# The last part of an output norm: engine order taken from tables, and its last tile accumulated onto the residual in PSUM

## Chip, cores and metric

The kernel runs on one core of one Trainium2 chip. The metric is the device time of one execution in microseconds, the median of several runs; smaller is better.

## What is computed

One layer of a streaming encoder: Mamba-2 heads beside latent attention heads, then a dense SwiGLU FFN, over 512 + 64 = 576 token columns of width 1024. Only its end matters here: the last down-projection of the FFN, the residual, and the final RMS norm.

```python
def rmsnorm(x, w):
    xf = x.astype(jnp.float32)
    y = xf * lax.rsqrt(jnp.mean(xf * xf, axis=-1, keepdims=True) + EPS)
    return (y * w.astype(jnp.float32)).astype(x.dtype)
...
# end of the layer:  y = rmsnorm(x + down(silu(gate) * up), final_gain)
```

The kernel holds activations transposed: 8 channel tiles t = 0..7 of 128 channels (partitions) by 576 tokens (columns). The mean over channels is therefore a sum over partitions and over the 8 tiles. Partitions are summed on TensorE (PE) with a matrix of ones.

## The kernel before

The FFN's 22 blocks of 128 hidden channels run through PE at nearly full occupancy. The last four blocks are projected down at the very end, and this end is cut in two parts of token columns: part 0 has columns 0 to 319 and part 1 columns 320 to 575 (`parts`). For each part and each tile t, `down_half` (L1101) issues 12 matmuls (4 blocks, each as three products of high and low halves of weight and activation) into one PSUM tile (`ps_l0_t` in part 0, `ps_l1_t` in part 1; the profile cuts both to `ps_l`). Then for each tile:

- VectorE (DVE) adds the PSUM tile to the residual in place, `add` (L1145): `x2[t] = ps + x2[t]`. In the rows x2 is `x`; `x2_0` holds the tiles 0 to 3, `x2_1` the tiles 4 to 7.
- ScalarE (ACT) squares it (L1184 in part 0, L1233 in part 1, result `sq`), and multiplies it in place by the norm's gain for that channel, `gain` (L1149). Tile 7 has no `gain`: its gain is multiplied in at the end.
- The squares are summed over tiles: in part 0 by GpSimd (POOL, L1189, tiles 0, 2, 4 into `ss`) and by DVE (L1194 into `sq_last`, joined to `ss` in two adds at L1192); in part 1 by POOL for the tiles 0 to 3 (L1238), while the tiles 4 to 7 are summed by PE itself, as `packed` (L1203) accumulates ones times `ss` and ones times each `sq` in PSUM.
- The norm's factor comes from `norm_steps` (L182 to L193): Ln, Exp and Square on ACT, three small operations on DVE. In part 0 the sum over partitions is the matmul at L1226; it stands behind tile 2 of part 1, and the factor is written back to PSUM (`ps_n`) and copied to SBUF (`R`, L1231). In part 1 the packed factor `Rp` is spread to all partitions by four matmuls (L1257, eight passes, result `ps_r`), with seven matmuls `ones` times `ones` (L1251, result unused) ahead of them, and one half is copied to SBUF (`R`, L1258).
- `outs` multiplies each tile by the factor: DVE (L1159; L1155 with the gain for tile 7), POOL for the tiles 0 and 1 of each part (L1157, factor from SBUF). The results are stored: part 0 from the SyncE (SP) queue in pairs, part 1 in single tiles by `SENDS`, four on SP and four on ACT's queue.

Two things set the order of work on an engine. Nearly all of the program is emitted in dependence order, and then tables of numbers (`ISSUE`, used in `issue_in_order`) give for PE, DVE, ACT, POOL and SP the order in which the emitted instructions are issued; tables called `PLACES` give the buffer that each tile takes. Part 1 stands in a block `tc.manual_schedule` (L1209) for PE, DVE, POOL and ACT: there these four engines issue in the order in which the code is written, and what the tables say of that stretch is just this order. Part 0 is under the tables.

Of the kernel before, what the change touches and what calls it, by code (L numbers as in the profile page):

```python
# [13 lines left out]
AF = mybir.ActivationFunctionType  # L14
ALU = mybir.AluOpType
# [4 lines left out]
P = 128  # L20
D = 1024
# [35 lines left out]
def hybrid_layer_kernel(ctx: ExitStack, tc: tile.TileContext, a, o):  # L57
# [54 lines left out]
    def col(c):  # L112
        return par[:, c : c + 1]
# [66 lines left out]
    def norm_steps(R, src, n, view=lambda z: z, eps=True):  # L180

        w = R.shape[1] if len(R.shape) == 2 else T  # L182
        y0, nv, u = (view(tmp(f"nr_{z}", w)) for z in "yvu")

        def first():
            act.activation(y0, src, AF.Ln, scale=1.0 / n, bias=epsb if eps else 0.0)
            dve.tensor_scalar(nv, src, -0.5 / n, -0.5 * EPS if eps else 0.0, ALU.mult, ALU.add)
            act.activation(y0, y0, AF.Exp, scale=-0.5)
            act.activation(u, y0, AF.Square)

        def second():
            dve.tensor_tensor(u, u, nv, ALU.mult)
            dve.scalar_tensor_tensor(R, u, 1.5, y0, ALU.add, ALU.mult)  # L193

        return first, second, nv
# [256 lines left out]
    def bank(tag, name):  # L452
        return placed(psq if tag == "sc" else psh, [P, 512], F32, tag, name)
# [646 lines left out]

    def down_half(ps, terms, cols, first=True, last=True):  # L1101
        for k, ((whi, wlo), (xhi, xlo)) in enumerate(terms):
            for i, (w, x) in enumerate(((whi, xhi), (whi, xlo), (wlo, xhi))):
                pe.matmul(  # L1104
                    ps, w, x[:, cols], start=first and k == 0 and i == 0, stop=last and k == len(terms) - 1 and i == 2,
                )
# [33 lines left out]
    def lbank(tag, name, i):  # L1140
        return bank(tag, name)[:, : parts[i].stop - parts[i].start]
# [9 lines left out]
    def outs(i, t, r, rp):  # L1151

        y = x2[t][:, parts[i]]
        if t == KT - 1:
            dve.scalar_tensor_tensor(y, y, col(C_NL + t), r, ALU.mult, ALU.mult)  # L1155
        elif t in POOLS[i]:
            pool.tensor_tensor(y, y, rp, ALU.mult)  # L1157
        else:
            dve.tensor_tensor(y, y, r, ALU.mult)  # L1159
# [35 lines left out]


    W1 = parts[1].stop - parts[1].start
    W2 = W1 // 2
# [9 lines left out]

    with tc.manual_schedule(engines={pe.engine, dve.engine, pool.engine, act.engine}):  # L1209
        pn0, pn1 = lbank("sc", "ps_n3_0", 0), bank("pp", "ps_n3_1")  # L1210
        first, second, _ = norm_steps(pn0, pn0, D, eps=False)
        q = []
        sent = [set(), set()]

        def out(i, k, r, rp):
            t = ORDERS[i][k]
            outs(i, t, r, rp)
            sent[i].add(t)
            if i == 0 and t ^ 1 in sent[i]:
                send(i, t & 6, 2, sp)  # L1220

        for t in range(KT):
            p = lbank(("hm", "sc", "pp")[t % 3], f"ps_l1_{t}", 1)
            down_half(p, last_terms(t), parts[1])
            if t == 2:
                pe.matmul(pn0, ones, ss3[:, parts[0]], start=True, stop=True)  # L1226
                first()
            add(t, 1, p)
            if t == 2:
                second()  # L1230
                act.copy(R3[:, parts[0]], pn0)  # L1231
            q.append(tmp("sq", W1))
            act.activation(q[t], x2[t][:, parts[1]], AF.Square)  # L1233
            if t < KT - 1:
                gain(t, 1)

            for k in {0: (), 1: (1, 0)}.get(t, (t,) if t < NP else ()):
                pool.tensor_tensor(ss3[:, parts[1]], ss3[:, parts[1]], q[k], ALU.add)  # L1238
            for k in OUTS.get(t, ()):
                out(0, k, pn0, R3[:, parts[0]])  # L1240
        packed(pn1, ss3[:, parts[1]], True, False)
        for t in range(NP, KT):
            packed(pn1, q[t], False, t == KT - 1)
        Rp = tmp("Rp", W2)
        first, second, _ = norm_steps(Rp, pn1[:, :W2], D, eps=False)
        first()
        second()

        warm = bank("hm", "ps_warm_last")
        for _ in range(7):  # L1250
            pe.matmul(warm[:, :P], ones, ones, start=True, stop=True)  # L1251

        pr1 = [lbank("sc", f"ps_r3_{z}", 1) for z in range(2)]
        for z in pr1:
            for hf in range(2):
                row = ident[:, 64 * hf : 64 * hf + 1].to_broadcast([P, P])
                pe.matmul(z[:, hf * W2 : (hf + 1) * W2], row, Rp, start=True, stop=True)  # L1257
        act.copy(R3[:, parts[1]], pr1[1])  # L1258
        for k in range(KT):
            out(1, k, pr1[0], R3[:, parts[1]])  # L1260
        for t, q in SENDS:
            send(1, t, 1, q)
    close(psH_)
# [10 lines left out]
def issue_in_order(tc, nc):  # L1274
# [26 lines left out]
    "sc": "".join("""  # L1301
021021202120120120120120120120120102102012102102102102121021021201201201201201210210210202102102021
""".split()),
    "pp": "".join("""
0210210212120102110201221002101210120121021012020120120120120120210210210210210210210210210210210210210210210210221012
0120210
""".split()),
# [130 lines left out]
4238 4170 4191 4198 4163 4192 4164 4193 4171-4172 4199 4165 4184 4200 4226 4173 4201 4174-4177 4239 4194 4227  # L1438
4207-4208 4228-4230 4240-4242 4202 4243 4231 4185 4209 4195 4262 4210 4186 4232 4211-4212 4263 4233 4213 4234 4214
4235 4244 4264 4203 4215 4223 4217 4204 4220 4245 4236 4218 4237 4216 4265-4266 4219 4224 4246 4267 4221 4225  # L1440
4250-4251 4268-4270 4247 4271 4252 4274 4253 4275 4254 4276-4277 4248 4255 4222 4278-4279 4272 4256 4249 4273
4257-4259 4280 4260-4261 4281-4391
""",
# [30 lines left out]
888 903 909 887 910 898-899 904 911 900 892 901 919 906 915 908 912 893 914 913 869 905 920-921 923 870 922 917 894  # L1474
918 924-925 916 895 928 902 927 937 926 929 896 938 932 931 939 930 933-934 940 935-936 941 946 942 944 943 945 947
951 949 948 954 950 952-953 955-979
""",
# [21 lines left out]
621 617-618 622 626 623 620 627-629 632 631 637 633-636 640 638-639 643 645 648 646 651 654 644 649 647 656 641 650  # L1499
657 655 659 658 663 660 642 661 664-665 652 666 662 674 667 669 653 675 670 668 677 676 671-672 686 673 684 680 678  # L1500
685 682 681 688-690 679 692 687 693-700 691 701-704 683 705-719
# [8 lines left out]
121 124-130 132 131 134 133 136 135 138 137 139-144 146 145 148 147 149-150 152 151 154 153 155-156 158 157 160 159  # L1510
161-169 171-172 170 175-176 174 177-181
""",
# [100 lines left out]
```

## Time and profile before

| quantity | value |
| --- | --- |
| median of 3 runs | 640.36 us (639.76 to 640.44) |
| the profiled execution's own time | 639.58 us |
| its span | 637.5 us |
| PE busy | 626.2 us (98% of the span) |
| DVE, ACT, POOL busy | 551.4, 390.4, 70.7 us |
| granted TensorE clock | 1.00 in the slices that hold part 0 and part 1 |

The span runs from the first to the last instruction of the execution; 639.58 - 637.5 = 2.08 us of the execution's own time lie around it. Times in a row of the timeline are counted from the start of the span: start, duration, engine, line, operation, result, sources, shapes, and in square brackets how long the engine had been idle before and what ended that. "x3" says that a row holds three instructions back to back. A duration contains the pipeline's fill, so the starts of rows lie closer together than their durations.

### The profile page before, as it was taken

Reading aid. Unit: us, or ns where it says so; the run is one execution under the profiler, and the core shown is the slowest. Engines: PE = TensorE matmul, PEld = TensorE weight load, DVE = VectorE, ACT = ScalarE, POOL = GpSimd, SP = SyncE. Lnnn points to the kernel's source line nnn. Section 1 sums busy time; section 2 is a strip of 40 time slices with the busy share of each in tenths; the row PEclk is TensorE's granted clock in tenths of the full one; section 3 lists DMA queues with packets and bytes.
Section 4 is the critical chain, followed back from the end, with each engine's and each line's share of the span. In section 5 each row is a group of like instructions: output and inputs, shape, how many; then the busy total and the mean of one; then the engine's idle time right before and its main releaser. Section 6 shows DMA issues by size and latency. Waiting matters only on the chain.

```text
span 637.5 us, 11950 instructions
## 1 busy us (share of the span) xinstructions
PE 626.2 (98%) x4639; PEld 598.0 (94%) x4639; DVE 551.4 (86%) x980; ACT 390.4 (61%) x751; POOL 70.7 (11%) x111
## 2 busy tenths in 40 slices
PE   9999999999999999999999999999999999999994
PEld 9899999985887899999999999999999999999994
DVE  6999996899867599999998997889888998998763
ACT  7655425789766479955656565655565656545463
POOL 1322122001010000000012002100211011100022
PEclk9999999999999999999999999999999999999999
DMA  9522185314131132231187427550765274723004
GB/s 310 207 51 78 35 209 151 114 30 147 72 111 34 62 131 73 93 108 67 36 202 158 128 91 163 141 136 40 189 159 133 67 182 111 181 74 133 1 1 149
DMA packets 31560, 72.66 MB, mean 114 GB/s; under 512 B 3706, under 2 KB 11400, under 8 KB 31248
## 3 DMA queue, kind: packets, MB, share of 16 engines
q1 hardware_dynamic: 25360, 60.77, 29.8%
q0 software_dynamic: 5424, 10.57, 9.3%
q8 instruction: 36, 0.59, 0.4%
q10 hardware_dynamic: 720, 0.57, 0.3%
q14 instruction: 20, 0.16, 0.1%
HBM read 58.03 MB, written 3.30 MB: 96 GB/s over the span
## 4 chain that ended last, share of the span: by engine, by line
PE 48%; issue 1%; DVE 1%; ACT 1%; POOL 1%; POOLq 0%; DVEq 0%
PE ps_x L894 17%; PE ps_dx L1034 9%; PE ps_z L894 9%; PE ps_dz L1034 5%; PE ps_y L894 4%; PE ps_dy L1034 2%; PE ps_l L1104 2%; POOL x L1157 0%; DVE x L1145 0%; DVE sq_last L1194 0%; DVE ss L1192 0%; POOL ss L1238 0%; POOLq L1600 0%; ACT sq L1233 0%; ACT x L1149 0%
## 5 line engine op out<-in xcount | busy, mean ns | idle before, releaser
L894 PE MATMUL ps_x<-xop,wh_gu_S 128*128 128x288 f32 x504 | 126.2, 295 | 0.0
L894 PEld LDWEIGHTS ps_x<-xop,wh_gu_S 128*128 128x128 f32 x504 | 88.2, 188 | 0.7 <-ACT u L963 0.2
L894 PE MATMUL ps_x<-xop,wl_gu_S 128*128 128x288 f32 x252 | 73.2, 295 | 0.0
L894 PE MATMUL ps_z<-xop,gu_a 128*128 128x288 f32 x252 | 61.7, 295 | 0.0
L127 ACT CAST wh_gu_S<-gu 128x1024 fp32r<-128x1024 f32 x44 | 46.2, 1053 | 14.8 <-PE ps_y L894 4.2
L128 DVE TENSOR_TENSOR wl_gu_S<-gu,wh_gu_S 128x1024 fp32r<-128x1024 f32 x44 | 52.8, 1217 | 0.8 <-ACT wh_gu_S L127 0.5
L894 PEld LDWEIGHTS ps_x<-xop,wl_gu_S 128*128 128x128 f32 x252 | 47.1, 188 | 0.0
L1047 POOL DMA_DIRECT2D x<-db x16 | 14.9, 930 | 277.9 <-ACT db L1040 247.8
L143 PE MATMUL ps_in<-xs,wh_in 128*128 128x288 f32 x256 | 45.5, 298 | 0.0
L894 PE MATMUL ps_y<-xop,wh_gu_A 128*128 128x288 f32 x168 | 44.9, 295 | 0.0
L894 PEld LDWEIGHTS ps_z<-xop,gu_a 128*128 128x128 f32 x252 | 43.5, 188 | 0.0
L894 PE MATMUL ps_z<-xop,wh_gu_S 128*128 128x288 f32 x168 | 43.4, 295 | 0.0
L894 PE MATMUL ps_x<-xop,wh_gu_A 128*128 128x288 f32 x168 | 42.7, 295 | 0.0
L143 PEld LDWEIGHTS ps_in<-xs,wh_in 128*128 128x128 f32 x256 | 37.8, 189 | 0.2
L127 ACT CAST wh_gu_A<-gu 128x1024 fp32r<-128x1024 f32 x22 | 23.1, 1051 | 23.0 <-PE ps_x L894 16.1
L894 PEld LDWEIGHTS ps_y<-xop,wh_gu_A 128*128 128x128 f32 x168 | 30.1, 188 | 0.1
L894 PEld LDWEIGHTS ps_z<-xop,wh_gu_S 128*128 128x128 f32 x168 | 29.7, 188 | 0.0
L128 DVE TENSOR_TENSOR wl_gu_A<-gu,wh_gu_A 128x1024 fp32r<-128x1024 f32 x22 | 26.8, 1217 | 3.3 <-ACT wh_gu_A L127 1.8
L894 PEld LDWEIGHTS ps_x<-xop,wh_gu_A 128*128 128x128 f32 x168 | 29.5, 188 | 0.0
L465 PE MATMUL ps_o<-cat_y,wh_out 128*128 128x288 f32 x128 | 29.0, 312 | 0.0
L143 PE MATMUL ps_in<-xs,wl_in 128*128 128x288 f32 x128 | 27.5, 296 | 0.0
L465 PE MATMUL ps_o<-cat_o,wh_out 128*128 128x288 f32 x128 | 27.3, 297 | 0.0
(594 smaller groups left out, 2002.8 us busy)
## 6 DMA issues: line engine op xcount, KB each, us to landing
gu<-in_w_gu SPq DMA_DIRECT2D x44, 512.0 KB, 4.8
db<-in_w_down SPq DMA_DIRECT2D x16, 512.0 KB, 4.5
x<-db POOLq DMA_DIRECT2D x16, 288.0 KB, 6.5
x<-dc POOLq DMA_DIRECT2D x16, 288.0 KB, 4.1
wr_in<-in_w_in SPq DMA_DIRECT2D x8, 512.0 KB, 6.2
wr_out<-in_w_out SPq DMA_DIRECT2D x8, 512.0 KB, 3.3
cumb<-cumD SPq DMA_DIRECT2D x5, 512.0 KB, 5.0
x<-in_xT SPq DMA_DIRECT2D x2, 1152.0 KB, 6.6
```

What stands on the lines that cost most here:

```text
L127: act.copy(hi, raw)
L128: dve.tensor_tensor(lo, raw, hi.bitcast(F32), ALU.subtract)
L143: pe.matmul(ps[:m, hf, :n], w, x[:, hf * n : (hf + 1) * n], start=start and k == 0 and i == 0, stop=stop and k == last and i == 2,)
L465: pe.matmul(ps[:, :n], w, x[:, cols], start=not onto and k == 0 and i == 0, stop=onto or (k == len(terms) - 1 and i == 2), skip_group_chec ...
L894: pe.matmul(ps, p, q, start=not onto and first and kp == kps[0] and j == 0, stop=onto or (last and kp == kps[-1] and j == 2), skip_group_c ...
L1034: pe.matmul(ps, l, r, start=not onto and k == 0 and j == 0, stop=onto or (k == n - 1 and j == 2), skip_group_check=onto,)
L1047: pool.dma_start(x2[t], v, accum_op=ALU.add)
L1104: pe.matmul(ps, w, x[:, cols], start=first and k == 0 and i == 0, stop=last and k == len(terms) - 1 and i == 2,)
```

## The change

Four edits, all in the last part of the program.

1. The `manual_schedule` block is gone. The tables of PE, DVE, ACT, POOL and SP now order that stretch too, and have other numbers from the start of part 0 on.
2. Tile 7 of part 1 is seeded: ACT copies the residual x2[7] into the tile's PSUM buffer (L1229), and the 12 matmuls accumulate onto it (`onto=True`: no matmul starts a new sum). ACT's Square (L1240) reads the sum from PSUM, and at the end DVE multiplies PSUM by the gain and by the factor's SBUF copy into the output (L1157). DVE's `add` of this tile is gone: DVE has 979 instructions instead of 980, ACT 720 instead of 719 beside the table loads. The tile's buffer is taken from the pool `pp`, not `sc`.
3. The factor of tile 7 is read from the copy `R` in SBUF, not from `ps_r`.
4. The seven unused matmuls multiply `ones` with the squares of tile 7 (`q[-1]`), and PE's table puts them behind the four that spread the factor.

Cut to its core:

```diff
-    def down_half(ps, terms, cols, first=True, last=True):
+    def down_half(ps, terms, cols, first=True, last=True, onto=False):
...
-                    ps, w, x[:, cols], start=first and k == 0 and i == 0, stop=last and k == len(terms) - 1 and i == 2,
+                    ps, w, x[:, cols], start=first and not onto and k == 0 and i == 0,
+                    stop=onto or (last and k == len(terms) - 1 and i == 2), skip_group_check=onto,
...
         if t == KT - 1:
-            dve.scalar_tensor_tensor(y, y, col(C_NL + t), r, ALU.mult, ALU.mult)
+            last = (y, r) if i == 0 else (seeded7[0], rp)
+            dve.scalar_tensor_tensor(y, last[0], col(C_NL + t), last[1], ALU.mult, ALU.mult)
...
-    with tc.manual_schedule(engines={pe.engine, dve.engine, pool.engine, act.engine}):
...
-            p = lbank(("hm", "sc", "pp")[t % 3], f"ps_l1_{t}", 1)
-            down_half(p, last_terms(t), parts[1])
+        seeded = t == KT - 1
+        p = lbank("pp" if seeded else ("hm", "sc", "pp")[t % 3], f"ps_l1_{t}", 1)
+        if seeded:
+            seeded7.append(p)
+            act.copy(p, x2[t][:, parts[1]])
+        down_half(p, last_terms(t), parts[1], onto=seeded)
...
-            add(t, 1, p)
+        if not seeded:
+            add(t, 1, p)
...
-            act.activation(q[t], x2[t][:, parts[1]], AF.Square)
+        act.activation(q[t], p if seeded else x2[t][:, parts[1]], AF.Square)
...
-            pe.matmul(warm[:, :P], ones, ones, start=True, stop=True)
+        pe.matmul(warm[:, :P], ones, q[-1][:, :P], start=True, stop=True)
...
     "POOL": """
-79 78 80-85 87 86 88-89 91 90 92-93 95 94 96-111
+79 78 80-85 87 86 88-89 91 90 92-93 95 94 96-109 111 110
```

Beside this, PE's table mixes the matmuls of different tiles: those of part 1 begin while part 0 is still under way, and the sum of part 0 (L1226, now L1232) stands behind 35 matmuls of part 1 (before: 36). On ACT the load of the function table stands ahead of the first Square of part 0. The lines below the change have moved by up to 11: L1145 is L1146, L1149 is L1150, L1159 is L1161, L1203 is L1206, L1233 is L1240, L1257 is L1264, L1251 is L1258.

**DVE, from the add of tile 3 of part 1 to the first step of part 1's norm.** Before (`ps_n3_0` is part 0's factor, `ps_n3_1` the packed sum of part 1, `ps_l1_t` tile t of part 1):

```order
L1145 TENSOR_TENSOR x2_0_2053<-ps_l1_3_7568,x2_0_2053 128x256
L1159 TENSOR_TENSOR x2_1_2055<-x2_1_2055,ps_n3_0_7501 128x320
L1145 TENSOR_TENSOR x2_1_2055<-ps_l1_4_7588,x2_1_2055 128x256
L1159 TENSOR_TENSOR x2_1_2055<-x2_1_2055,ps_n3_0_7501 128x320
L1159 TENSOR_TENSOR x2_0_2053<-x2_0_2053,ps_n3_0_7501 128x320
L1145 TENSOR_TENSOR x2_1_2055<-ps_l1_5_7610,x2_1_2055 128x256
L1159 TENSOR_TENSOR x2_0_2053<-x2_0_2053,ps_n3_0_7501 128x320
L1159 TENSOR_TENSOR x2_1_2055<-x2_1_2055,ps_n3_0_7501 128x320
L1145 TENSOR_TENSOR x2_1_2055<-ps_l1_6_7630,x2_1_2055 128x256
L1155 SCALAR_TENSOR_TENSOR x2_1_2055<-x2_1_2055,par_81,ps_n3_0_7501 128x320
L1145 TENSOR_TENSOR x2_1_2055<-ps_l1_7_7649,x2_1_2055 128x256
L187 TENSOR_SCALAR nr_v_7677<-ps_n3_1_7502 128x128
```

Now:

```order
L1146 TENSOR_TENSOR x2_0_2053<-ps_l1_3_7566,x2_0_2053 128x256
L1161 TENSOR_TENSOR x2_1_2055<-x2_1_2055,ps_n3_0_7499 128x320 x2
L1161 TENSOR_TENSOR x2_0_2053<-x2_0_2053,ps_n3_0_7499 128x320 x2
L1146 TENSOR_TENSOR x2_1_2055<-ps_l1_4_7586,x2_1_2055 128x256
L1161 TENSOR_TENSOR x2_1_2055<-x2_1_2055,ps_n3_0_7499 128x320
L1146 TENSOR_TENSOR x2_1_2055<-ps_l1_5_7608,x2_1_2055 128x256
L1146 TENSOR_TENSOR x2_1_2055<-ps_l1_6_7628,x2_1_2055 128x256
L1157 SCALAR_TENSOR_TENSOR x2_1_2055<-x2_1_2055,par_81,ps_n3_0_7499 128x320
L187 TENSOR_SCALAR nr_v_7675<-ps_n3_1_7500 128x128
```

Four outputs of part 0 now stand together ahead of the add of tile 4, and no add of tile 7 stands ahead of the norm.

**ACT, from the Squares of part 1's last tiles to the copy of its factor.** Before (`nr_y`, `nr_u` are the norm's steps, `R1` the factor's copy; L1149 is the gain):

```order
L1233 ACTIVATE sq_7644<-x2_1_2055 128x256
L1149 ACTIVATE x2_1_2055<-x2_1_2055,par_81 128x256
L1233 ACTIVATE sq_7663<-x2_1_2055 128x256
L186 ACTIVATE nr_y_7676<-ps_n3_1_7502 128x128
L188 ACTIVATE nr_y_7676<-nr_y_7676 128x128
L189 ACTIVATE nr_u_7678<-nr_y_7676 128x128
L1258 COPY R1_99<-ps_r3_1_7694 128x256
```

Now:

```order
L1240 ACTIVATE sq_7642<-x2_1_2055 128x256
L1240 ACTIVATE sq_7661<-ps_l1_7_7647 128x256
L1150 ACTIVATE x2_1_2055<-x2_1_2055,par_81 128x256
L186 ACTIVATE nr_y_7674<-ps_n3_1_7500 128x128
L188 ACTIVATE nr_y_7674<-nr_y_7674 128x128
L189 ACTIVATE nr_u_7676<-nr_y_7674 128x128
L1150 ACTIVATE x2_0_2053<-x2_0_2053,par_81 128x256 x3
L1150 ACTIVATE x2_1_2055<-x2_1_2055,par_81 128x256 x2
L1265 COPY R1_99<-ps_r3_1_7692 128x256
```

Five gains have moved from among the Squares to the place between the norm's Square and the copy of the factor; the Square of tile 7 reads PSUM.

**PE, the end of its program.** Before (`sq_7644` and `sq_7663` hold the squares of the tiles 6 and 7, `ps_r3_0` and `ps_r3_1` the spread factor):

```order
L1203 MATMUL ps_n3_1_7502<-sq_7644,ones_86 64x128 x2
L1203 MATMUL ps_n3_1_7502<-sq_7663,ones_86 64x128 x2
L1251 MATMUL ps_warm_last_7685<-ones_86 128x128 x7
L1257 MATMUL ps_r3_0_7693<-Rp_7675,ident_84 128x128 x2
L1257 MATMUL ps_r3_1_7694<-Rp_7675,ident_84 128x128 x2
```

Now:

```order
L1206 MATMUL ps_n3_1_7500<-sq_7642,ones_86 64x128 x2
L1206 MATMUL ps_n3_1_7500<-sq_7661,ones_86 64x128 x2
L1264 MATMUL ps_r3_0_7691<-Rp_7673,ident_84 128x128 x2
L1264 MATMUL ps_r3_1_7692<-Rp_7673,ident_84 128x128 x2
L1258 MATMUL ps_warm_last_7683<-sq_7661,ones_86 128x128 x7
```

The seven unused matmuls have changed places with the four that spread the factor.

**DVE, the sums of squares of part 0.** Before (`ps_l0_t` is tile t of part 0, `sq_last` collects the squares of DVE's tiles, `ss3` is what the ones matmul reads):

```order
L1194 TENSOR_TENSOR sq_last_7356<-sq_last_7356,sq_7423 128x320
L1145 TENSOR_TENSOR x2_1_2055<-ps_l0_5_7445,x2_1_2055 128x320
L1145 TENSOR_TENSOR x2_1_2055<-ps_l0_7_7481,x2_1_2055 128x320
L1145 TENSOR_TENSOR x2_1_2055<-ps_l0_6_7463,x2_1_2055 128x320
L1194 TENSOR_TENSOR sq_last_7356<-sq_last_7356,sq_7459 128x320
L1145 TENSOR_TENSOR x2_0_2053<-ps_l1_0_7506,x2_0_2053 128x256
L1194 TENSOR_TENSOR sq_last_7356<-sq_last_7356,sq_7477 128x320
L1192 TENSOR_TENSOR ss3_3201<-ss3_3201,sq_last_7356 128x320
L1192 TENSOR_TENSOR ss3_3201<-ss3_3201,sq_7495 128x320
```

Now:

```order
L1146 TENSOR_TENSOR x2_1_2055<-ps_l0_5_7445,x2_1_2055 128x320
L1146 TENSOR_TENSOR x2_1_2055<-ps_l0_6_7463,x2_1_2055 128x320
L1196 TENSOR_TENSOR sq_last_7356<-sq_last_7356,sq_7423 128x320
L1196 TENSOR_TENSOR sq_last_7356<-sq_last_7356,sq_7459 128x320
L1146 TENSOR_TENSOR x2_1_2055<-ps_l0_7_7481,x2_1_2055 128x320
L1196 TENSOR_TENSOR sq_last_7356<-sq_last_7356,sq_7477 128x320
L1194 TENSOR_TENSOR ss3_3201<-ss3_3201,sq_last_7356 128x320
L1194 TENSOR_TENSOR ss3_3201<-ss3_3201,sq_7495 128x320
```

The first two sums come behind the adds of the tiles 5 and 6, and the add of part 1's tile 0 no longer stands among them.

More of the change, by code (lines that the diff above doesn't have):

```diff
@@ L1207, in done @@
             yield lambda: outs(i, t, r, rp)
-    with tc.manual_schedule(engines={pe.engine, dve.engine, pool.engine, act.engine}):
[L1210 to L1222, printed above, removed]
-            p = lbank(("hm", "sc", "pp")[t % 3], f"ps_l1_{t}", 1)
-            down_half(p, last_terms(t), parts[1])
-            if t == 2:
-                pe.matmul(pn0, ones, ss3[:, parts[0]], start=True, stop=True)
-                first()
-            add(t, 1, p)
[L1229 to L1262, printed above, removed]
@@ new lines, in hybrid_layer_kernel @@
+    packed(pn1, ss3[:, parts[1]], True, False)
+    for t in range(NP, KT):
+        packed(pn1, q[t], False, t == KT - 1)
+    Rp = tmp("Rp", W2)
+    first, second, _ = norm_steps(Rp, pn1[:, :W2], D, eps=False)
+    first()
+    second()
+    warm = bank("hm", "ps_warm_last")
+    for _ in range(7):
+        pe.matmul(warm[:, :P], ones, q[-1][:, :P], start=True, stop=True)
+    pr1 = [lbank("sc", f"ps_r3_{z}", 1) for z in range(2)]
+    for z in pr1:
+        for hf in range(2):
+            row = ident[:, 64 * hf : 64 * hf + 1].to_broadcast([P, P])
+            pe.matmul(z[:, hf * W2 : (hf + 1) * W2], row, Rp, start=True, stop=True)
@@ L1263, in hybrid_layer_kernel @@
+    act.copy(R3[:, parts[1]], pr1[1])
+    for k in range(KT):
+        out(1, k, pr1[0], R3[:, parts[1]])
+    for t, q in SENDS:
+        send(1, t, 1, q)
     close(psH_)
```

51 lines of the change are left out of this document (40 added, 11 removed).

## The prediction

> **What bounds the kernel now.** I read the page's head and its busy times first, then the windows of the last 20 us, the chain of waits at its end, and the timeline of each engine there.
>
> ```profile
> span 637.5 us, 11950 instructions
> PE 626.2 (98%) x4639; PEld 598.0 (94%) x4639; DVE 551.4 (86%) x980; ACT 390.4 (61%) x751; POOL 70.7 (11%) x111
> ```
>
> PE sets the time nearly everywhere: 98% of the span. A change of the program's end can only win what PE loses there, or what follows PE's last useful work.
>
> ```profile
> 612.00:624.70 12.70, 12.54 (x101) 12.05 (x100) 9.36 (x22) 10.77 (x26) 7.28 (x9) 1.00 0.08 27
> 624.70:632.10 7.40, 4.64 (x43) 3.60 (x42) 4.58 (x14) 3.17 (x9) 1.77 (x3) 1.00 0.53 179
> ```
>
> The columns are stretch, length, busy time of PE, weight loads, DVE, ACT and POOL, granted clock, share of DMA, GB/s. Up to 624.70 PE is full but for 0.16 us (12.70 - 12.54); from there to 632.10 no engine is: 7.4 us of a serial chain (norm of part 1, factor, outputs). The chain of waits ends so:
>
> ```profile
> 623.34 1.72 POOL x L1157 x2
> 625.06 5.58 issue
> 630.64 0.76 POOLq L1600
> 631.40 0.69 POOL x L1157
> ```
>
> The last compute on it is POOL's second output of part 1, ending at 631.40 + 0.69 = 632.09. To the end of the span are 637.5 - 632.09 = 5.41 us (stores and the program's close), and 2.08 us lie around the span: 637.5 + 2.08 = 639.58. I take these 7.49 us as unchanged: each queue still sends four stores of part 1, only the one behind POOL's last output now goes out from SP (tile 0) and not from ACT (tile 1). So I sum how much earlier POOL's last output ends.
>
> **The change, part by part.**
>
> *(a) The last matmul of part 1.* PE's only loss in part 1 is at the ones matmul of part 0:
>
> ```profile
> 616.32 0.28 PE L1104 MATMUL ps_l<-pr,wl_dl 128*128 128x256 f32 x1
> 616.75 0.81 PE L1226 MATMUL ps_n<-ss,ones 128*128 128x320 f32 x2 [0.16 <-DVE ss L1192]
> ...
> 624.22 0.40 PE L1104 MATMUL ps_l<-pr,wh_dl 128*128 128x256 f32 x2
> 624.46 0.28 PE L1104 MATMUL ps_l<-pr,wl_dl 128*128 128x256 f32 x1
> ```
>
> From 624.22 to 624.46 two matmuls were started: 0.12 us each. At 616.32 the next start should have been 616.44; it was 616.75: 0.31 us lost to a late `ss`. Why late:
>
> ```profile
> 613.57 0.85 DVE L1194 TENSOR_TENSOR sq_last<-sq_last,sq 128x320 f32<-128x320 f32 x1
> 614.67 0.83 DVE L1194 TENSOR_TENSOR sq_last<-sq_last,sq 128x320 f32<-128x320 f32 x1
> 616.21 0.49 DVE L1192 TENSOR_TENSOR ss<-ss,sq 128x320 f32<-128x320 f32 x1
> 611.96 3.19 POOL L1189 TENSOR_TENSOR ss<-ss,sq 128x320 f32<-128x320 f32 x3 [60.16 <-ACT sq L1184]
> 609.39 1.28 ACT L1127 ACT_TABLE_LOAD   x1
> 610.69 0.47 ACT L1184 ACTIVATE sq<-x 128x320 f32<-128x320 f32 x1
> ```
>
> Two of DVE's sums took 0.85 and 0.83 us where the same shape takes 0.49 with POOL idle; both lie inside POOL's own sums (611.96 to 615.15). So the two engines get in each other's way when both read only SBUF. In the new order the table load (1.28 us) stands ahead of ACT's Squares, in time that ACT waits anyway, so POOL's sums start about 1.3 us sooner, and DVE's first two sums come later, behind the adds of tiles 5 and 6. I expect both collisions, 0.36 + 0.34 = 0.70 us, to go, more than the 0.31 needed. The bounds are 0 (a collision stays) and 0.31 (all of it); the mixing of matmuls gives nothing itself, PE was full. The two collisions are the nearer case: **-0.3**.
>
> *(b) From the last matmul to the Ln of part 1's norm.*
>
> ```profile
> 624.67 0.44 PE L1203 MATMUL ps_n<-ss,ones 128*64 128x128 f32 x4
> 624.94 0.61 PE L1203 MATMUL ps_n<-sq,ones 128*64 128x128 f32 x8
> 625.98 0.44 PE L1203 MATMUL ps_n<-sq,ones 128*64 128x128 f32 x4 [0.43 <-ACT sq L1233]
> 626.82 0.44 PE L1203 MATMUL ps_n<-sq,ones 128*64 128x128 f32 x4 [0.41 <-ACT sq L1233]
> ...
> 623.53 0.49 DVE L1159 TENSOR_TENSOR x<-x,ps_n 128x320 f32<-128x320 f32 x1 [1.40 <-ACT x L1149]
> 624.26 0.87 DVE L1159 TENSOR_TENSOR x<-x,ps_n 128x320 f32<-128x320 f32 x2
> 625.06 0.42 DVE L1145 TENSOR_TENSOR x<-ps_l,x 128x256 f32<-128x256 f32 x1
> 625.85 0.41 DVE L1145 TENSOR_TENSOR x<-ps_l,x 128x256 f32<-128x256 f32 x1
> ...
> 626.37 0.40 ACT L1233 ACTIVATE sq<-x 128x256 f32<-128x256 f32 x1
> 627.31 0.28 ACT L186 ACTIVATE nr_y<-ps_n 128x128 f32<-128x128 f32 x1 [0.54 <-PE ps_n L1203]
> ```
>
> Tile 7's last matmul ends at 624.46 + 0.28 = 624.74; its add starts only at 625.85, since DVE's queue is behind: an output of part 0 waited 1.40 us for ACT's gain, and outputs and adds follow it in line. Then Square at 626.37, the last packed passes at 626.82, Ln at 627.31. From 624.74 that is 2.57 us. Now neither DVE nor a gain stands between. ACT squares the seeded tile where it is: start 0.05 us after its last matmul (as Ln after the last packed pass, 626.82 + 0.44 to 627.31), 0.40 long, 0.05 to PE, 0.44 for the four passes of this tile, 0.05 to Ln: 0.99. PE has 20 packed passes in all: 8 in a row took 0.61 and 4 took 0.44, so 0.04 each and 0.28 of fill; started at 624.67, that is 0.07 before the matmul's end, they run for 0.28 + 20 x 0.04 = 1.08, and Ln follows at 1.08 - 0.07 + 0.05 = 1.06. PE is the later one. The adds of tiles 4 to 6 must be done too: with the stall of 1.40 gone from the queue, four outputs ahead of add 4 need 4 x 0.42 and no add ends later than tile 7's matmuls; I allow 0.13 for their Squares queueing on ACT ahead of tile 7's: 1.19. **-1.4** (2.57 - 1.19 = 1.38). No row shows ACT squaring a 256-column PSUM tile; its Ln of PSUM (128x128, 0.28) is no longer than one of its shape from SBUF (0.31, the Square at 628.02 quoted below), so I take nothing extra for PSUM; the bounds are no queueing on ACT (-1.5) and a Square that takes twice as long and so becomes the later path, 0.99 + 0.40 + 0.13 = 1.52 (-1.05).
>
> *(c) From Ln to POOL's end.*
>
> ```profile
> 628.02 0.31 ACT L189 ACTIVATE nr_u<-nr_y 128x128 f32<-128x128 f32 x1
> 622.53 0.96 ACT L1149 ACTIVATE x<-x,par 128x256 f32<-128x256 f32 x2
> 625.96 0.51 ACT L1149 ACTIVATE x<-x,par 128x256 f32<-128x256 f32 x1
> 629.03 1.16 PE L1257 MATMUL ps_r<-Rp,ident 128*128 128x128 f32 x8
> 630.23 0.37 ACT L1258 COPY R<-ps_r 128x256 f32<-128x256 f32 x1 [1.90 <-PE ps_r L1257]
> 630.68 1.41 POOL L1157 TENSOR_TENSOR x<-x,R 128x256 f32<-128x256 f32 x2 [5.62 <-ACT R L1258]
> 631.45 0.47 DVE L1155 SCALAR_TENSOR_TENSOR x<-x,par,ps_r 128x256 f32<-128x256 f32 x1
> ```
>
> With T = 627.31, Square starts at T + 0.71, PE's factor passes at T + 1.72, the copy at T + 2.92, POOL ends at 632.09 = T + 4.78. Now five gains stand between Square and copy. Two back to back took 0.96 and one takes 0.51, so the second costs 0.45, and the last of five ends 0.51 + 4 x 0.45 = 2.31 after the first starts. If that first one starts 0.2 to 0.3 after Square does, the copy can start at about T + 0.95 + 2.31 - 0.1 (the overlap of a row with the next) = T + 3.15 instead of T + 2.92. So the cover of the gains, PE's 1.16 us and the wait of 1.90 before the copy, is just too short: **+0.2**, bounds 0 and +0.4. Tile 7's output on DVE now needs the copy too and has one output behind it; DVE ended at 631.45 + 0.47 = 631.92, and with copy at T + 3.15 it ends about T + 3.15 + 0.37 + 0.47 + 0.42 = T + 4.4, ahead of POOL's T + 5.0. The gains that moved serve outputs that wait for PE's passes (T + 2.88) anyway; the fifth, at T + 3.2, serves an output that DVE reaches after 3 others of 0.4. Nothing lost.
>
> *(d) The seed.* ACT's copy of 256 columns (0.37, as the copy at 630.23) must be there before PE's first matmul of tile 7. Behind it on PE is everything: PE issues in order. ACT reaches the copy behind part 0's Ln, Exp and Square and one more Square of part 1:
>
> ```profile
> 618.89 0.47 ACT L189 ACTIVATE nr_u<-nr_y 128x320 f32<-128x320 f32 x1
> 617.56 1.57 POOL L1238 TENSOR_TENSOR ss<-ss,sq 128x256 f32<-128x256 f32 x2 [2.41 <-ACT sq L1233]
> 619.39 0.49 DVE L192 TENSOR_TENSOR nr_u<-nr_u,nr_v 128x320 f32<-128x320 f32 x1 [0.18 <-ACT nr_u L189]
> ```
>
> This Square ends at 619.36, 2.6 us after the ones matmul's start at 616.75. Then one Square (0.42) and the copy (0.37): some 3.4 us after the ones matmul. In the new order 29 matmuls stand on PE between that matmul and tile 7's first: 29 x 0.12 = 3.5, and the ones matmul's own two passes, which I put at half of their 0.81: 3.9. So about 0.5 us of cover; cost nothing, bounds 0 and, with every ACT step 0.1 late, +0.1.
>
> Sum: -0.3 - 1.4 + 0.2 = **-1.5**. Profiled 639.58 becomes 638.1; from the median 640.36, 0.78 above the profiled one, **638.8**.
>
> **Rivals.**
>
> *1, port collisions come back elsewhere.* The sums of part 1 on POOL (1.57 for two, 0.75 to 0.8 each) now fall beside DVE's two steps of part 0's norm, which have two SBUF sources (the L192 row, and L193 behind it). If each waits as at 613.57 (0.85 - 0.49 = 0.36), the factor of part 0 is 0.7 us late, its outputs push the adds of tiles 4 to 6, and of (b) 0.7 goes: -0.8, 639.6. For it: these operations are neighbours in the new order. Against: (b) has its largest part from tile 7 alone, which no longer passes DVE. The Trainium skill, page "SBUF — State Buffer", section "SBUF: two separate sides", has this as an exclusive lock on a port pair: a DVE operation with two SBUF sources and a POOL operation that reads SBUF block each other for the whole instruction. By that rule each step could wait for a whole POOL sum, 2 x 0.78 = 1.56, and the gain would be nil; the trace agrees that they collide, but shows 0.36.
>
> *2, PE's passes of the factor slow down.* The unused matmuls (PE busy from 627.19 to 629.03) now stand behind the factor's passes, and PE is idle for about 1.7 us (T to Rp) ahead of them. What a cold PE costs is at the program's start:
>
> ```profile
> 1.07 3.78 PE L218 MATMUL ps_warm<-ones 128*128 128x128 f32 x16 [1.07 <-POOL nepsb L110]
> 627.19 1.83 PE L1251 MATMUL ps_warm_last<-ones 128*128 128x128 f32 x14
> ```
>
> 3.78 / 16 = 0.236 against 1.83 / 14 = 0.131 for the same pass: 1.8 times. Then 1.16 becomes 2.09, of which the gains hide 0.2: +0.7, net -0.8, again 639.6. Against: the clock read 1.00 in both windows, and PE's idle 0.43 and 0.41 ahead of packed passes left these at 0.44 both times. The Trainium skill, page "TensorE: Matmul & The Clock Gate", Part 1 on the HAM clock gate, has the rate halve only after a whole window of some 3.4 us without work; by that rule this rival doesn't happen and the sum stays at -1.5; no run here yet shows it.
>
> *3, the end doesn't follow POOL.* If the stores or the close are bound by something older, the tail's gain is not passed on: 0 to -0.3, 640.2. Against: the chain ends with POOL's output, 0.76 us of its queue before it.
>
> *4, slower: the seed comes late.* If part 0's sum of squares is late (collision kept and L1226's successor waits), ACT's seed is late by the same, and PE stands at tile 7's first matmul with all remaining work behind it: every us is lost one for one. The cover is 0.5 us by (d) and the gain 1.5, so it decides from a delay of 2.0 us on; with 3.5 us (the norm of part 0 waiting for the Squares of part 1 that the new order mixes in, some eight instructions of 0.42) it gives +1.5, 641.9.
>
> **How the numbers follow.** Forecast 0.62; rival 1 0.14, rival 2 0.09, rival 3 0.07, rival 4 0.08. Around the forecast, the bounds go from -0.31 - 1.5 + 0 = -1.8 to about -0.9 (the upper ends of (b) and (c) with half of (a)): 638.5 to 639.4. The runs of before spread by 0.34 to each side; with it, and to hold 8 in 10, the range takes in rivals 1 and 2 and stops short of 3 and 4: **638.1 to 639.9**. A difference under 0.2% (1.28 us, or beyond 639.08 and 641.64) can't be told from no change in this measurement. The forecast itself lies 0.28 below that line, so a part of its chance, some 0.08, counts as same: faster 0.56 (0.54 of the forecast, the rest from rivals that cost less than thought), same 0.36, slower 0.08.
>
> **What would show it.** Right: Ln of part 1 about 1.2 us after the last matmul of tile 7; the ones matmul of part 0 without a wait; DVE's `sq_last` sums at 0.49; the factor's copy on ACT released by the gains, not by PE; 8 passes of the factor in about 1.16. Wrong: sums or norm steps of 0.8 us on DVE beside POOL (rival 1), passes above 0.2 us (rival 2), POOL's end early but the span not (rival 3), a gap on PE ahead of tile 7's first matmul (rival 4). The forecast fails if one of the three terms has the wrong sign.

## The result

The changed kernel's median is **638.29 us** (637.74 to 639.25, 14 runs) against 639.89 us of the kernel before in the same sessions (14 runs); the ratio is 0.9974 with a 95% interval of 0.9966 to 0.9982. By the ratio that is 0.26% or 1.66 us (1.15 to 2.18) faster; the two medians differ by 1.60. The profiled execution took 637.74 us, its span 635.8.

The page's head and the windows of the changed kernel's end (columns as before):

```profile
span 635.8 us, 11955 instructions
PE 625.1 (98%) x4639; PEld 597.3 (94%) x4639; DVE 551.1 (87%) x979; ACT 389.6 (61%) x752; POOL 70.3 (11%) x111
```

```profile
612.00:624.20 12.20, 12.20 (x99) 11.92 (x97) 10.05 (x23) 8.77 (x22) 5.12 (x7) 1.00 0.15 52
624.20:630.50 6.30, 4.04 (x43) 3.60 (x42) 3.18 (x10) 4.07 (x12) 1.41 (x2) 1.00 0.50 167
```

PE has no hole left ahead of its last matmul (12.20 of 12.20 us), and the stretch from its end to the end of POOL's last output, in which no engine is full, has shrunk from 7.4 to 6.1 us. PE there, with both places at which it had lost time before:

```profile
616.11 0.28 PE L1104 MATMUL ps_l<-pr,wl_dl 128*128 128x256 f32 x1
616.23 0.75 PE L1232 MATMUL ps_n<-ss,ones 128*128 128x320 f32 x2
624.00 0.28 PE L1104 MATMUL ps_l<-pr,wl_dl 128*128 128x256 f32 x1
624.21 0.44 PE L1206 MATMUL ps_n<-ss,ones 128*64 128x128 f32 x4
624.48 1.04 PE L1206 MATMUL ps_n<-sq,ones 128*64 128x128 f32 x16
627.29 1.16 PE L1264 MATMUL ps_r<-Rp,ident 128*128 128x128 f32 x8 [1.77 <-DVE Rp L193]
```

The ones matmul of part 0 (L1232) starts 0.12 us behind its neighbour, without a wait. The 20 packed passes (L1206) run in one piece, 624.21 to 625.52. The factor's 8 passes take 1.16 us as before, after 1.77 us of idle PE. The other engines:

```profile
612.66 1.09 DVE L1196 TENSOR_TENSOR sq_last<-sq_last,sq 128x320 f32<-128x320 f32 x2
614.45 0.48 DVE L1196 TENSOR_TENSOR sq_last<-sq_last,sq 128x320 f32<-128x320 f32 x1
619.18 0.92 DVE L193 SCALAR_TENSOR_TENSOR ps_n<-nr_u,nr_y 128x320 f32<-128x320 f32 x1
618.78 0.38 ACT L1229 COPY ps_l<-x 128x256 f32<-128x256 f32 x1
624.32 0.38 ACT L1240 ACTIVATE sq<-ps_l 128x256 f32<-128x256 f32 x1
625.57 0.28 ACT L186 ACTIVATE nr_y<-ps_n 128x128 f32<-128x128 f32 x1 [0.47 <-PE ps_n L1206]
626.49 2.09 ACT L1150 ACTIVATE x<-x,par 128x256 f32<-128x256 f32 x5
628.49 0.37 ACT L1265 COPY R<-ps_r 128x256 f32<-128x256 f32 x1
628.94 1.41 POOL L1159 TENSOR_TENSOR x<-x,R 128x256 f32<-128x256 f32 x2 [5.50 <-ACT R L1265]
```

ACT copies the seed at 618.78, squares tile 7 from PSUM at 624.32, 0.04 us after its last matmul (624.00 + 0.28), and starts Ln at 625.57. The five gains behind the norm's Square take 2.09 us and end just as the copy of the factor can start. The chain of waits still ends with POOL's second output, now at 629.67 + 0.68 = 630.35:

```profile
623.44 5.47 issue
628.90 0.76 POOLq L1611
629.67 0.68 POOL x L1159
```

From there to the span's end are 635.8 - 630.35 = 5.45 us (5.41 before).

The profiled executions reach part 0 at different times (first column, 601.55 to 603.33), though the program up to there is the same; so the table below compares the end alone, from the end of PE's last gate or up matmul (its row in the kernel before is 601.43 + 0.29) to the end of POOL's last output. All numbers are starts or ends of rows of the timeline, in us; "way" is the last column minus the first. The kernels e1 to e9 are the experiments of the next section. One profiled execution, the first of e8, took 1570 us, with matmuls of about twice their length (128x288: 565 ns on average, 295 in the changed kernel), so the row of e8 below is from its second session.

| kernel | last gate/up ends | last matmul of part 1 ends | Ln starts | POOL's last ends | to last matmul | from it to Ln | Ln to POOL's end | way |
| --- | --- | --- | --- | --- | --- | --- | --- | --- |
| before | 601.72 | 624.74 | 627.31 | 632.09 | 23.02 | 2.57 | 4.78 | 30.37 |
| after | 601.64 | 624.28 | 625.57 | 630.35 | 22.64 | 1.29 | 4.78 | 28.71 |
| e1 | 602.69 | 625.72 | 627.41 | 632.18 | 23.03 | 1.69 | 4.77 | 29.49 |
| e2 | 603.19 | 625.84 | 627.29 | 632.07 | 22.65 | 1.45 | 4.78 | 28.88 |
| e3 | 601.55 | 624.57 | 627.10 | 631.89 | 23.02 | 2.53 | 4.79 | 30.34 |
| e4 | 602.44 | 625.10 | 627.67 | 632.44 | 22.66 | 2.57 | 4.77 | 30.00 |
| e5 | 602.17 | 624.83 | 626.52 | 631.30 | 22.66 | 1.69 | 4.78 | 29.13 |
| e6 | 601.55 | 624.19 | 626.30 | 631.09 | 22.64 | 2.11 | 4.79 | 29.54 |
| e7 | 603.33 | 625.98 | 627.27 | 632.05 | 22.65 | 1.29 | 4.78 | 28.72 |
| e8 | 602.90 | 625.55 | 626.62 | 631.46 | 22.65 | 1.07 | 4.84 | 28.56 |
| e9 | 602.07 | 624.74 | 626.18 | 630.97 | 22.67 | 1.44 | 4.79 | 28.90 |

The change's way is 1.66 us shorter: 0.38 up to the last matmul, 1.28 from there to Ln, nothing behind it. The intervals of whole times are 0.1% to 0.15% (0.6 to 1 us) to each side, so a single edit is told by this table and only the sums by the times.

### The profile page after: what moved, and what is told of

Its sections match the earlier page's. It is cut to its first block, busy times and chain, and to the rows that moved or that the text cites. A ratio compares the mean times of both kernels' runs of the same rounds, so it can differ in the third digit from the quotient of the medians.

```text
span 635.8 us, 11955 instructions
## 1 busy us (share of the span) xinstructions
PE 625.1 (98%) x4639; PEld 597.3 (94%) x4639; DVE 551.1 (87%) x979; ACT 389.6 (61%) x752; POOL 70.3 (11%) x111
## 4 chain that ended last, share of the span: by engine, by line
PE 90%; DVE 5%; DMA 2%; issue 1%; ACT 1%; POOL 0%; SPq 0%; POOLq 0%; DVEq 0%; ACTq 0%
PE ps_x L894 21%; PE ps_z L894 10%; PE ps_dx L1034 9%; PE ps_in L143 8%; PE ps_o L465 7%; PE ps_y L894 5%; PE ps_dz L1034 5%; PE ps_z L465 4%; PE ps_l L1104 3%; PE ps_dy L1034 2%; PE ps_first L143 2%; PE ps_p L894 2%; PE sc L680 2%; PE pv L727 1%; PE ptp L702 1%
```

## The experiments

Two theories were set against each other. **Q**: the gain is that of a queue cleared on ACT and DVE in front of tile 7's add, that is, of the order tables. **S**: it is that of the seed, which takes add and residual off the last tile's path. "Made" numbers in the diffs are places in ACT's table: 673 is the load of the function table, 683 the part-0 gain of tile 2, 693 and 695 the Squares of part 1's tiles 0 and 1, 706, 708 and 710 the part-1 gains of tiles 4, 5 and 6.

**e1, the late gain early.** One row of the kernel before is moved in ACT's table, by thirteen places (the expectation's seven is a miscount):

```diff
-... 692 687 693-700 691 701-704 683 705-719
+... 692 687 683 693-700 691 701-719
```

> The kernel before, with one row moved in ACT's order: the part-0 gain of tile 2 (L1149) stands seven rows earlier in the part-0 stretch, ahead of the first Square of part 1, where ACT had 0.49 us idle. Before, it ran at about 622.98 and a part-0 output on DVE waited 1.40 us for it. Theory Q (the gain came from clearing the queue in front of tile 7's add): the wait of 1.40 goes, tile 7's add starts right behind its last matmul (about 624.8 instead of 625.85), Ln of part 1 at about 626.2 instead of 627.31, and the time is 1.0 us (0.9 to 1.2) below the kernel before. Theory S (the seed itself brings it): 0 to -0.3 us.

Measured: time ratio 0.9995 (0.9985 to 1.0005), way -0.88 us. DVE's and ACT's rows at the end:

```profile
624.88 0.54 DVE L1155 SCALAR_TENSOR_TENSOR x<-x,par,ps_n 128x320 f32<-128x320 f32 x1
625.75 0.42 DVE L1145 TENSOR_TENSOR x<-ps_l,x 128x256 f32<-128x256 f32 x1 [0.34 <-PE ps_l L1104]
626.06 0.51 ACT L1149 ACTIVATE x<-x,par 128x256 f32<-128x256 f32 x1
626.47 0.40 ACT L1233 ACTIVATE sq<-x 128x256 f32<-128x256 f32 x1
627.41 0.28 ACT L186 ACTIVATE nr_y<-ps_n 128x128 f32<-128x128 f32 x1 [0.54 <-PE ps_n L1203]
```

DVE's add of tile 7 (625.75) is now released by PE and not by the queue, as Q has it. But its Square waits for ACT until 626.47, because ACT is still at tile 6's gain: ACT's chain of Squares and gains has become the bound. So Ln comes 1.69 us after the last matmul, not the 1.46 that Q gave (626.2 less 624.74), and still 0.88 us sooner than before. The whole time can't confirm it: -0.88 us is 0.9986, within its interval.

**e2, the change without the seed.** The changed kernel and its tables; tile 7 as all others:

```diff
-            act.copy(p, x2[t][:, parts[1]])
-        down_half(p, last_terms(t), parts[1], onto=seeded)
+        down_half(p, last_terms(t), parts[1])
...
-        if not seeded:
-            add(t, 1, p)
+        add(t, 1, p)
...
-        act.activation(q[t], p if seeded else x2[t][:, parts[1]], AF.Square)
+        act.activation(q[t], x2[t][:, parts[1]], AF.Square)
```

> The changed kernel with its order tables, but without the seed: DVE adds tile 7 to the residual behind its last part-0 output, ACT squares it from SBUF, the last output takes its factor from PSUM as before. Theory Q: DVE and ACT are free when tile 7's last matmul ends, so add (0.41), Square (0.4) and the last 4 packed passes only just outlast the 16 passes that PE runs meanwhile; Ln of part 1 is 0.1 to 0.2 us later after the last matmul than with the seed (1.29), and the time about 1.5 us below the kernel before. Theory S: the add is back on the path at its whole price with its place in the queue, 0.8 us or more are lost, and the time is at most 0.9 us below the kernel before.

Measured: ratio 0.9975 (0.9963 to 0.9987), way 28.88, 0.17 us longer than with the seed.

```profile
625.88 0.42 DVE L1146 TENSOR_TENSOR x<-ps_l,x 128x256 f32<-128x256 f32 x1
626.34 0.42 ACT L1235 ACTIVATE sq<-x 128x256 f32<-128x256 f32 x1 [0.40 <-DVE x L1146]
627.29 0.28 ACT L186 ACTIVATE nr_y<-ps_n 128x128 f32<-128x128 f32 x1
```

Add and Square follow the last matmul (ending at 625.84) without a queue, and Ln comes 1.45 us after it instead of 1.29. S is out: with the new order in place, the seed is worth 0.16 us of 1.66.

**e3, the seed without the new order.** The changed kernel's code with the tables of the kernel before; the seed's copy (711) stands in ACT's table behind the third step of part 0's norm:

```diff
-... 693-699 700 691 701-704 683 705-719
+... 693-699 711 700 691 701-704 683 705-710 712-720
```

> The seed alone: the changed kernel's code with the order of the kernel before on every engine; ACT's seed copy stands ahead of the copy of part 0's factor, where ACT waited 1.09 us, and tile 7's add is gone from DVE. Theory Q: tile 7's Square still stands on ACT behind tile 6's Square and gain, which wait for the delayed add of tile 6, so Ln of part 1 stays within 0.1 us of 627.31 and the time within 0.2 us of the kernel before. Theory S: Ln about 1.1 us or more earlier, the time 1 us or more below.

Measured: ratio 1.0000 (0.9989 to 1.0011), way -0.03 us.

```profile
625.78 0.51 ACT L1150 ACTIVATE x<-x,par 128x256 f32<-128x256 f32 x1
626.20 0.36 ACT L1240 ACTIVATE sq<-ps_l 128x256 f32<-128x256 f32 x1
627.10 0.28 ACT L186 ACTIVATE nr_y<-ps_n 128x128 f32<-128x128 f32 x1 [0.54 <-PE ps_n L1206]
```

Tile 7's sum is in PSUM at 624.57, yet its Square starts at 626.20, right behind tile 6's gain: by itself the seed brings nothing, since ACT's queue holds the tile back whichever way it comes.

**e4, the table load first.**

```diff
-... 671-672 686 673 684 ...
+... 671-673 686 684 ...
```

> The kernel before with one row moved on ACT: the load of the function table (1.28 us) stands ahead of the first Square of part 0. By step (a) of the prediction POOL's three sums start about 1.3 us earlier, DVE's two sums of 0.85 and 0.83 us become 0.49, the ones matmul of part 0 starts without its wait, the last matmul ends 0.3 us earlier and the time is 0.3 us (0.2 to 0.4) lower. Rival: the sums collide at other places, or the order of DVE's sums counts and not the load: the ones matmul still waits, the time stays within 0.1 us.

Measured: ratio 0.9993 (0.9982 to 1.0005), way -0.37 us, all of it ahead of the last matmul.

```profile
617.03 0.28 PE L1104 MATMUL ps_l<-pr,wl_dl 128*128 128x256 f32 x1
617.15 0.77 PE L1226 MATMUL ps_n<-ss,ones 128*128 128x320 f32 x2
614.28 0.48 DVE L1194 TENSOR_TENSOR sq_last<-sq_last,sq 128x320 f32<-128x320 f32 x1
615.02 0.84 DVE L1194 TENSOR_TENSOR sq_last<-sq_last,sq 128x320 f32<-128x320 f32 x1
614.30 1.21 POOL L1189 TENSOR_TENSOR ss<-ss,sq 128x320 f32<-128x320 f32 x1
```

The ones matmul follows at 0.12 us, without its wait. Of DVE's two long sums one is back at 0.48: it started 0.02 us ahead of POOL's third sum (614.30), and here it is POOL's that took longer, 1.21 us where one takes 0.88 undisturbed. The other still takes 0.84, having started before that sum ended (615.51), and it didn't matter. So step (a) holds with this edit alone, and taking one of the two delays off DVE was enough.

**e5, both rows moved.** The edits of e1 and e4 together.

> The kernel before with the two rows moved on ACT's order together: the late part-0 gain of tile 2 and the load of the function table. Alone, the first shortened the stretch from the last matmul to Ln from 2.57 to 1.69 us, the second ended the last matmul 0.36 us earlier. Theory Q: the two are independent, so both show again and the sum is 1.2 us (1.1 to 1.4), about three quarters of the change's gain without any seed, added instruction or other table. Rival: they share the same slack on ACT (the early gain takes time that the early Squares need), and the sum is under 1.0.

Measured: ratio 0.9986 (0.9974 to 0.9998), way -1.24 us, the sum of -0.88 and -0.37.

```profile
624.55 0.28 PE L1104 MATMUL ps_l<-pr,wl_dl 128*128 128x256 f32 x1
626.52 0.28 ACT L186 ACTIVATE nr_y<-ps_n 128x128 f32<-128x128 f32 x1 [0.54 <-PE ps_n L1203]
```

Ln again follows the last matmul (624.83) by 1.69 us. Two rows of one table bring three quarters of the change.

**e6, the gains back among the Squares.** In the changed kernel:

```diff
-... 694 705 707 709 712 706 713-715 702 704 696 710 708 716-720
+... 694 705-710 712-715 702 704 696 716-720
```

> The changed kernel, with the part-1 gains of the tiles 4, 5 and 6 back among the Squares of part 1 on ACT, one behind each Square, as in the kernel before. Theory Q: ACT then needs about 0.45 us more for each, tile 7's Square starts at about 1.1 us after its last matmul instead of 0.04, Ln comes 0.6 to 0.9 us later than in the changed kernel (1.29 after the last matmul), and nothing is won behind it, since the copy of the factor waits for PE's 8 passes at the same moment as for the gains. Rival: ACT has slack between the adds (0.74 and 0.31 us of idle), the gains hide in it, and Ln moves by less than 0.2 us.

Measured: ratio 0.9976 (0.9963 to 0.9990), way 29.54, 0.83 us longer than in the changed kernel (with that, 0.9987 would be expected; the interval holds it).

```profile
624.98 0.51 ACT L1150 ACTIVATE x<-x,par 128x256 f32<-128x256 f32 x1
625.39 0.36 ACT L1240 ACTIVATE sq<-ps_l 128x256 f32<-128x256 f32 x1
626.30 0.28 ACT L186 ACTIVATE nr_y<-ps_n 128x128 f32<-128x128 f32 x1 [0.54 <-PE ps_n L1206]
629.22 0.37 ACT L1265 COPY R<-ps_r 128x256 f32<-128x256 f32 x1 [0.70 <-PE ps_r L1264]
```

Tile 7's Square starts 1.20 us after its last matmul (624.19) behind three gains, and Ln 0.82 us later than in the changed kernel. The copy of the factor then waits 0.70 us for PE: the gains cost nothing there and 0.82 here.

**e7, no collision beside part 0's norm.** In the changed kernel the Square of part 1's tile 0 (693) moves behind the copy of part 0's factor (700), so that POOL starts its sums later:

```diff
-... 695 697-699 693 711 701 700 703 ...
+... 695 697-699 711 701 700 693 703 ...
```

> The changed kernel, with the Square of tile 0 of part 1 moved on ACT behind the copy of part 0's factor, so that POOL's sums of part 1 begin after DVE's last step of part 0's norm (L193) and not beside it. In the changed kernel that step took 0.92 us beside POOL's sums where it took 0.50 before. Theory: it is the two engines' SBUF reads that collide, so L193 is back at 0.50 and the factor's copy is 0.4 us earlier; but the adds of the tiles 4 to 6 wait for PE then, so Ln stays at 1.29 (1.2 to 1.35) after the last matmul. Rival 1 of the prediction: the collision cost the end some 0.4 us, and Ln comes that much earlier.

Measured: one time, 639.54 us, beside which nothing can be told of 0.4 us; way 28.72 (28.71).

```profile
620.88 0.50 DVE L193 SCALAR_TENSOR_TENSOR ps_n<-nr_u,nr_y 128x320 f32<-128x320 f32 x1
624.10 0.42 DVE L1146 TENSOR_TENSOR x<-ps_l,x 128x256 f32<-128x256 f32 x1 [0.39 <-PE ps_l L1104]
627.27 0.28 ACT L186 ACTIVATE nr_y<-ps_n 128x128 f32<-128x128 f32 x1 [0.47 <-PE ps_n L1206]
```

DVE's last step of part 0's norm is back at 0.50 us (0.92 in the changed kernel, L193). The 0.42 us so won come out as 0.39 us of waiting for PE ahead of tile 4's add: this stretch is hidden behind PE's matmuls. Ln stays at 1.29.

**e8, 16 packed passes.** In the changed kernel POOL sums the squares of tile 4 too, and PE packs four pairs:

```diff
-    NP = 4
+    NP = 5
...
-    packed(pn1, ss3[:, parts[1]], True, False)
-    for t in range(NP, KT):
-        packed(pn1, q[t], False, t == KT - 1)
+    packed(pn1, q[5], True, False)
+    packed(pn1, q[6], False, False)
+    packed(pn1, ss3[:, parts[1]], False, False)
+    packed(pn1, q[7], False, True)
```

> The changed kernel, with the squares of tile 4 summed by POOL as well (one more sum, behind its part-0 outputs), so PE has 16 packed passes and not 20; the pairs of the tiles 5 and 6 come first, then the sum of POOL, then tile 7. The 20 passes took 1.31 us and are what now lies between the last matmul and Ln; tile 7's own path through Square is shorter. Theory: Ln comes at 1.1 us (1.05 to 1.15) after the last matmul instead of 1.29, and the end with it. Rival: POOL's added sum ends after 624.9 in the changed kernel's time and PE waits for it, so Ln stays or comes later.

> The kernel of e8 once more, since its profiled execution fell into a disturbed state in which even matmuls outside the change took more than twice as long. Theory as before: with 16 packed passes and not 20, Ln comes 1.1 us (1.05 to 1.15) after the last matmul instead of 1.29, and POOL's last output 0.2 us earlier. Rival: PE waits for POOL's added sum, and Ln stays at 1.29 or comes later.

Measured: ratio 0.9977 (0.9962 to 0.9992) and in the second session 0.9983 (0.9969 to 0.9998), way 28.56.

```profile
625.48 0.66 PE L1206 MATMUL ps_n<-sq,ones 128*64 128x128 f32 x8
625.96 0.39 PE L1206 MATMUL ps_n<-ss,ones 128*64 128x128 f32 x4
626.18 0.39 PE L1206 MATMUL ps_n<-sq,ones 128*64 128x128 f32 x4
624.75 0.74 POOL L1245 TENSOR_TENSOR ss<-ss,sq 128x256 f32<-128x256 f32 x1
626.62 0.28 ACT L186 ACTIVATE nr_y<-ps_n 128x128 f32<-128x128 f32 x1 [0.25 <-PE ps_n L1206]
```

POOL's added sum ends at 625.49 and PE takes it up at 625.96 without a wait; Ln comes 1.07 us after the last matmul instead of 1.29. Of these 0.22 us, 0.06 are lost behind Ln (4.84 instead of 4.78). The way is the shortest of all, by 0.15 us; its time can't be told from the changed kernel's.

**e9, three moves on ACT.** The order of the kernel before on the other engines, no seed; on ACT the moves of e1 and e4, and the gains of tiles 4 to 6 behind the Square of part 1's norm:

```diff
-... 672 686 673 684 ... 687 693-700 691 701-704 683 705-719
+... 672-673 686 684 ... 687 683 693-700 691 701-705 707 709 711-714 706 708 710 715-719
```

> Order of the kernel before on PE, DVE, POOL and SP, no seed, and three moves on ACT alone: the late part-0 gain of tile 2 early (e1), the table load first (e4), and the part-1 gains of the tiles 4 to 6 behind the Square of part 1's norm. Theory Q: from e1, ACT's chain of Squares and gains is what holds tile 7's Square; without those gains the add follows the last matmul at once, Square follows the add, and Ln comes 1.45 us (1.4 to 1.5) after the last matmul, as in e2; with e4's 0.36 the way from the last gate/up matmul to POOL's last output is 28.9 us (28.8 to 29.0) against 30.37 before and 28.71 in the changed kernel: all but the seed's 0.16 us from three moves on one engine. Rival: the tables of PE and DVE have their own part in it (outputs in a row, mixed matmuls), and the way stays above 29.1.

Measured: ratio 0.9986 (0.9971 to 1.0000), way 28.90, 1.47 us shorter than before.

```profile
624.77 0.42 DVE L1146 TENSOR_TENSOR x<-ps_l,x 128x256 f32<-128x256 f32 x1 [0.34 <-PE ps_l L1104]
625.23 0.42 ACT L1235 ACTIVATE sq<-x 128x256 f32<-128x256 f32 x1 [0.80 <-DVE x L1146]
626.18 0.28 ACT L186 ACTIVATE nr_y<-ps_n 128x128 f32<-128x128 f32 x1 [0.54 <-PE ps_n L1205]
```

Add, Square and Ln follow the last matmul (624.74) as in e2. The tables of PE and DVE, with their mixed matmuls and outputs in a row, have no part in it that shows: e2, which has them, needs 28.88. Nor has the new place of the seven unused matmuls: they stand ahead of the factor's passes in e9 and behind them in e2, and from Ln to POOL's end it is 4.79 and 4.78.

## Why the prediction was right

The forecast was 1.5 us; the way is 1.66 us shorter, and so is the time by the ratio. The median lies 0.5 us below the 638.8 forecast mainly because the kernel before, too, came out lower in these sessions (639.89 and not 640.36). The places at which time was won were forecast; what wins most of it was not, and slips in (b) and (c) offset each other in part. One sum of the range is off: the upper ends of (b) and (c) with half of (a) are -1.05 + 0.4 - 0.15 = -0.8, not -0.9. The steps:

- *(a), -0.3.* Measured -0.38, and e4 shows that the table load's place alone does -0.36. Of it 0.31 us are the wait; most of the rest is that the ones matmul keeps PE from its next start for 616.58 - 616.23 = 0.35 us instead of 617.16 - 616.75 = 0.41. That both of DVE's collisions had to go was not so: e4 kept one. Nor do both lie inside POOL's sums: the second starts there and ends 0.35 us behind them.
- *(b), -1.4.* Measured -1.28. The stretch is PE's 20 packed passes, as worked out, but these took 1.31 us and not 1.08: a pass is 0.05 us apart from the next, not 0.04. The 0.13 us allowed for queueing on ACT weren't needed, which by luck covers half of that slip. What was wrong is where the gain was put. "(b) has its largest part from tile 7 alone, which no longer passes DVE" is refuted: the seed is 0.16 us of it (e2), and nothing alone (e3). The late part-0 gain is 0.88 (e1), and the gains taken out from among the Squares are 0.25 (1.69 in e5 to 1.44 in e9). These shares hold for the moves in this order: put back in the changed kernel, three of the gains cost 0.82 (e6). The wait of 1.40 us was named in the prediction; that its removal leaves ACT's own chain as the next bound was not, and e1 fell short of Q by it.
- *(c), +0.2.* Measured 0.00. Five gains took 2.09 us with the first at 0.50, so 0.40 for each further one. The 0.45 came from a misread row: the two gains at 622.53 of the kernel before were one of 256 columns and one of 320, the late part-0 gain itself, in a row that names only the first shape. The gains and PE's passes ended together (628.58 and 628.45, the copy at 628.49), so the copy wasn't held by the gains, as the prediction had it.
- *(d), nothing.* The seed ended at 619.16. At 0.12 us per matmul from 617.05 on, PE reached tile 7's first one at about 620.3, so the cover was 1.1 us, more than the 0.5 worked out.
- *Rival 1* came true in part and cost nothing: L193 took 0.92 us beside POOL, and e7 shows that PE's matmuls hide it. *Rival 2* didn't happen in the changed kernel's profile: the factor's passes took 1.16 us after 1.77 us of idle PE, and the clock read 1.00. But e6 shows that the shortness of the gap doesn't secure this. There the passes also took 1.16 us after 1.77 us of idle PE (628.02 to 629.18); then the granted clock (third figure from the right in the window's row) fell, to 0.78 on average in 629.00:629.50 and 0.50 in 630.00:632.00, and the 14 passes of the unused matmuls took 2.95 us where they take 1.73 in the changed kernel:

```profile
629.02 2.95 PE L1258 MATMUL ps_warm_last<-sq,ones 128*128 128x128 f32 x14
630.00:632.00 2.00, 1.97 (x10) 1.67 (x8) 0.98 (x3) 0.00 (x0) 1.08 (x2) 0.50 0.94 310
```

The average of 0.78 puts the fall at 629.28, 0.10 us behind the factor's last pass. The Trainium skill's page "TensorE: Matmul & The Clock Gate" (Part 1, the HAM clock gate) has the rate halve only after a whole window of some 3.4 us without work; e6's trace doesn't agree, since PE was busy for 1.64 of the 3.41 us ahead of the fall (625.87:629.28). With the unused matmuls ahead of the passes (before, e9) PE has no such gap. Whether in some executions of the changed kernel the fall comes before the passes, no run here tells, since each profile shows one execution.

- *Rival 3* fell: in all eleven profiles of the table the span ends 5.40 to 5.46 us after POOL's last output, wherever that lies. *Rival 4*: no hole on PE.

## What to carry to other kernels

When a tail waits on an in-order queue, look first for the instruction in it that is early work done late: one gain moved up by thirteen places was over half of this gain, while the rewrite that took the last tile's add away was a tenth, and nothing without the new order. After each such move read which engine releases the next step; here DVE's queue, ACT's chain and PE's packed passes were the bound one after the other, and only the first two were worth an edit. A grouped row can hold two shapes under the name of one; where a price is taken from it, look at the instructions apart.

## What was not expected of the hardware

What a collision of DVE and POOL costs. POOL's single operations are needed to see it, since longer windows merge them (the first row is from the kernel before, the second from the changed one; they end at 615.16 and 619.74):

```profile
614.15 1.01 POOL L1189 TENSOR_TENSOR ss<-ss,sq 128x320 f32<-128x320 f32 x1
618.97 0.77 POOL L1245 TENSOR_TENSOR ss<-ss,sq 128x256 f32<-128x256 f32 x1 [1.08 <-ACT sq L1240]
```

| DVE's operation | starts | POOL's, under way, ends | DVE's ends | longer than alone |
| --- | --- | --- | --- | --- |
| first long sum, before | 613.57 | 614.07 | 614.42 | 0.37 |
| second long sum, before | 614.67 | 615.16 | 615.51 | 0.35 |
| long sum, e4 | 615.02 | 615.51 | 615.86 | 0.36 |
| L193, after | 619.18 | 619.74 | 620.10 | 0.42 |

All four of DVE's operations end 0.35 to 0.36 us behind the end of the POOL operation that was under way when they started, so each waited for that operation. The Trainium skill's page "SBUF — State Buffer" (SBUF: two separate sides) has the port pair held for the whole instruction by the operation that starts first; these rows agree, and e4's third sum of POOL, which took 1.21 us behind a DVE sum that started 0.02 us earlier, shows the same the other way round. e7 agrees that the overlap is the cause, since L193 falls from 0.92 to 0.50 us once POOL's sums begin after it. So 0.36 us is no fixed price, as the prediction took it to be against this rule: it depends on how much of POOL's operation is left, here 0.5 to 0.6 us each time. The dearest case, a DVE operation that starts just behind a POOL operation, no run here shows.
